# A hybrid encoder on one Trainium2 core: conv taps into PSUM, and a new order and engine table for the mixer's steps

## The chip, the cores and the metric

One core of one Trainium2 chip. The time is device microseconds of one launch; lower is better. Before the change three runs gave 2029.0, 2029.43 and 2029.79 us, median 2029.43.

## The reference

`x` is 512 tokens by 1024 channels, and there are two layers. Each layer does

```
x += 1/2 SwiGLU_1(RMSNorm(x))                       # d_ff 2816
h  = RMSNorm(x) @ W_in                              # 1696 columns
y  = concat[ MLA(h_mla), Conv(h_conv), Hyena(h_hy) ] # each group RMS-normalised
x += y @ W_out
x += 1/2 SwiGLU_2(RMSNorm(x))
```

MLA is attention with 8 heads over latent projections (softmax over 512 keys). Conv is `a * sigmoid(g)`, a depthwise convolution of 31 taps over 256 channels, a layer norm and a silu. Hyena is a depthwise convolution of 3 taps over 768 channels, then two long filters as products with spectra, each followed by a gate. A last RMSNorm ends it. All is float32.

## The kernel before

Channels lie on partitions and the 512 tokens on the free axis, so `x` is eight tiles of 128x512. Float32 products are made from parts: a matrix is split into a rounded part `hi` (a cast on ScalarE, L327) and a remainder `lo` (a subtraction on VectorE, L301, or on GpSimd, L331), and a product is three TensorE passes, hi·hi, hi·lo and lo·hi (`mm3`, L366 to L368). Each weight tile is loaded raw by SyncE's queue (`load_w`, `wr`), then cast (`wh`) and subtracted (`wl`).

The program is written as a list of operations. `Plan.issue` (L176) is a list scheduler: it runs a clock over modelled costs, gives each engine the ready operation that was written first, and lets a tile take a buffer only when one is free. The order that results is fixed for each engine, and on the chip each engine works through its own list in order, waiting at semaphores. The costs are those in `v_tt`, `v_stt`, `act`, `p_tt`, `mm` and so on (L299 to L383); each engine counts for itself. PSUM is one tag, `ps`, of 8 banks. Other work tiles share one tag of 61 slots.

`mixer` (L818) writes its steps in the order of `MIX_ORDER` (L30). `C` makes a half of the conv's input (two `W_in` tiles, then `upad`), `H` one of Hyena's six input tiles with its short convolution (`short_conv`, L697), `K`, `Q`, `KV`, `W` and `V` the latents of attention, `S` a head's scores and softmax, `P` its values, `Y` a piece of the long filters (`long_conv`, L706), `T` a number of conv taps (`conv_taps`, L774), `CF` and `HF` the norms of the conv and Hyena groups, `OM` and `OR` the two halves of the output projection, which add into `x`.

Of the 62 first-stage taps of a layer, 33 run on VectorE (2 `v_ts` that start `cacc` and 31 `v_stt` that add into it, all in SBUF); the other 29, those in `POOL_TAPS`, are a ScalarE scaling into `tap` (L322) and a GpSimd addition (L331). Hand-made tables (`POOL_W`, `POOL_Y`, `POOL_WIN`, `ACT_NORM` and so on, L33 to L40) say which other operations go to GpSimd or ScalarE.

Of the kernel before, what the change touches and what calls it, by code (L numbers as in the profile page):

```python
# [19 lines left out]
P = 128  # L20
# [28 lines left out]
# columns of the packed per-layer vectors  # L49
# [8 lines left out]
# columns of the packed constants  # L58
# [6 lines left out]
class Tile:  # L65
    """a tile that is allocated when the first operation that writes it is issued"""
# [10 lines left out]
class View:  # L77
    """a tile, or an access pattern of DRAM, behind a chain of slices that is applied when it is issued"""
# [44 lines left out]
class Op:  # L123
    """one step of the program"""

    __slots__ = ("engine", "cost", "emit", "succ", "n_pred", "ready", "index", "allocs", "tiles", "table", "late", "prio", "start", "end",
                 "crit")
# [5 lines left out]
class Plan:  # L133
    def __init__(self, nc):
        self.nc, self.ops, self.tags, self.prio = nc, [], {}, 0
# [5 lines left out]
    def add(self, engine, cost, emit, reads, writes, table=None, late=0.0, after=()):  # L141
        op = Op()
        op.engine, op.cost, op.emit, op.table, op.late = engine, cost, emit, table, late
# [30 lines left out]
        self.ops.append(op)  # L174

    def issue(self):  # L176
        """list schedule by rank among what is ready; a tile leaves a slot for every earlier tile of its tag"""
        events, ready, seq = [], {}, 0
# [22 lines left out]
        while done < len(self.ops):  # L201
# [15 lines left out]
            for engine, heap in ready.items():  # L217
# [24 lines left out]
                end = now + cost  # L242
                op.start, op.end = now, end
# [19 lines left out]
def trunk(ctx: ExitStack, tc: tile.TileContext, a: dict, out: bass.AP):  # L263
# [35 lines left out]
    def v_tt(o, x0, x1, op):  # L299
        plan.add("DVE", 0.07 + o.free * 1.04e-3,  # L300
                 lambda: nc.vector.tensor_tensor(out=g(o), in0=g(x0), in1=g(x1), op=op), rd(x0, x1), [o])  # L301

    def v_ts(o, x0, s1, s2_, op0, op1=None):
        c = 1.1e-3 if x0.in_psum else 0.52e-3
        kw = {} if op1 is None else {"op1": op1}
        plan.add("DVE", 0.07 + o.free * c + 0.06 * len(rd(s1, s2_)),
                 lambda: nc.vector.tensor_scalar(out=g(o), in0=g(x0), scalar1=g(s1), scalar2=g(s2_), op0=op0, **kw),  # L307
                 rd(x0, s1, s2_), [o])

    def v_stt(o, x0, s, x1, op0, op1):  # L310
        plan.add("DVE", 0.07 + o.free * 1.04e-3 + 0.06 * len(rd(s)),
                 lambda: nc.vector.scalar_tensor_tensor(out=g(o), in0=g(x0), scalar=g(s), in1=g(x1), op0=op0, op1=op1),  # L312
                 rd(x0, s, x1), [o])

    def v_copy(o, x0):
        plan.add("DVE", 0.07 + o.free * (1.04e-3 if x0.in_psum else 0.52e-3),
                 lambda: nc.vector.tensor_copy(g(o), g(x0)), rd(x0), [o])
# [11 lines left out]
    def p_tt(o, x0, x1, op):  # L329
        plan.add("POOL", 0.06 + o.free * 2.3e-3,  # L330
                 lambda: nc.gpsimd.tensor_tensor(out=g(o), in0=g(x0), in1=g(x1), op=op), rd(x0, x1), [o])  # L331

    def p_ts(o, x0, s1, s2_, op0, op1):
        plan.add("POOL", 0.06 + o.free * 1.3e-3,
                 lambda: nc.gpsimd.tensor_scalar(out=g(o), in0=g(x0), scalar1=g(s1), scalar2=g(s2_), op0=op0, op1=op1),
                 rd(x0, s1, s2_), [o])

    def p_pow(o, x0, x1):
        plan.add("POOL", 1.0, lambda: nc.gpsimd.tensor_tensor(out=g(o), in0=g(x0), in1=g(x1), op=ALU.pow),  # L339
                 rd(x0, x1), [o])  # L340
# [11 lines left out]
    def mm(o, lhs, rhs, start, stop, passes=4):  # L352
        plan.add("PE", rhs.free * passes / 2.4e3 + 0.003,
# [5 lines left out]
    def mm3(o, pairs):  # L359
        """sum of lhsT.T @ rhs over (lhs_hi, lhs_lo, rhs_hi, rhs_lo), three passes each"""  # L360
# [10 lines left out]
        for i, p in enumerate(pairs):  # L371
            plan.add("PE", 3 * (p[2].free / 2.4e3 + 0.003), emit(i, *p), list(p), [o])

    def mm2(o, pairs):
        """sum of lhsT.T @ (rhs_hi + rhs_lo) over (lhs, rhs_hi, rhs_lo)"""
# [34 lines left out]
    def load_w(src, width, pool_lo=False):  # L410
        """raw weights [128, width] to their f32r parts"""
# [3 lines left out]
        (p_tt if pool_lo else v_tt)(lo[:, :width], raw[:, :width], hi[:, :width].f, ALU.subtract)  # L415
# [5 lines left out]
    def stat(t, n, eps):  # L421
        """sum over partitions / n + eps, as [token % 128, token // 128]"""
# [9 lines left out]
    def bcast(c, n=4):  # L432
        """[128, n] by token to a PSUM row of 128 n in every partition"""
# [14 lines left out]
    def squares(tiles):  # L448
        acc = None
        for t in tiles:  # L450
# [4 lines left out]
            else:  # L455
                p_tt(acc, acc, sq, ALU.add)
        return acc

    class Norm:
        """takes x tiles as they become final; gives the split x * g and the row 1 / rms"""  # L460
# [3 lines left out]
        def __init__(self, l, name):  # L464
            self.l, self.name, self.xh, self.xl, self.acc, self.squared = l, name, [], [], None, 0

        def add(self, k, square=True):
# [4 lines left out]
            self.xh.append(h)  # L472
            self.xl.append(lo)
# [3 lines left out]
        def square(self, k):  # L477
            self.squared = k + 1
# [4 lines left out]
            else:  # L483
                p_tt(self.acc, self.acc, sq, ALU.add)

        def pairs(self, wt):
            return [(h, lo, self.xh[k], self.xl[k]) for k, (h, lo) in enumerate(ktiles(wt, KD))]

        def row(self):
            for k in range(self.squared, KD):  # L490
                self.square(k)
            return rstd_row(self.acc, D)

    def reduce_angle(t):
        """t to [-pi, pi], in place"""
# [27 lines left out]
    def down_in_halves(src, gh, gl, nxt):  # L523
        """the last product, by halves of the tokens; the weights stay for the second one"""
# [27 lines left out]
    def ffn(l, which, nrm, nxt, filler=None, first=None):  # L552
# [3 lines left out]
        def evac(pg, pu, gh, gl):  # L556
# [5 lines left out]
            p_tt(s, s, rb[0], ALU.mult)  # L562
# [30 lines left out]
    def spectra(l, res):  # L593
        """puts (ka, kc, inv) into res: spectra [block][order] of [j, kind, channel] and 1 / (512 sum |k|) by channel"""
# [12 lines left out]
        def packed(t):  # L607
            """t, twice in its rows, as [hi; lo]"""
# [27 lines left out]
        for par_ in range(2):  # L636
# [7 lines left out]
            for c in range(2):  # L644
# [10 lines left out]
                for op in (ALU.add, ALU.subtract):  # L655
                    t, th, tl = s2(s="sd"), s2(F32R, "sh"), s2(F32R, "sl")
                    p_tt(t, fb[0], fb[1], op)
# [5 lines left out]
                p_tt(fb[0], fb[0], fb[1], ALU.add)  # L663
                if ch:
                    p_tt(nrm, nrm, fb[0], ALU.add)
# [40 lines left out]
    def long_conv(l, o, u, gate, spec, res):  # L706
        """puts gate * (u (*) k + d u) for the two channel tiles into res"""
        ka, kc, iv = spec
        xp = [ps(), ps()]
        for t in range(2):  # L710
# [3 lines left out]
            p_tt(ue, up, dn_, ALU.add)  # L714
            v_tt(uo[:, 0::2], up[:, 0::2], dn_[:, 0::2], ALU.subtract)
            v_tt(uo[:, 1::2], dn_[:, 1::2], up[:, 1::2], ALU.subtract)
# [7 lines left out]
        wh, wl = [], []  # L724
        for jb in range(2):
# [11 lines left out]
            p_tt(m1.halves(), m1.halves(), m2.halves()[:, ::-1], ALU.subtract)  # L737
            v_tt(m3, ab, kcj, ALU.mult)
            v_tt(m4.halves(), cd.halves(), kaj.halves()[:, ::-1], ALU.mult)
            p_tt(m3.halves(), m3.halves(), m4.halves()[:, ::-1], ALU.add)  # L740
            w0, w1 = s2(s="w"), s2(s="w")
            (p_tt if 2 * o + jb in POOL_W0 else v_tt)(w0[:, 0:256], m1[:, 0:256], m1[:, 256:512], ALU.add)
            v_tt(w0[:, 256:512], m1[:, 0:256], m1[:, 256:512], ALU.subtract)
            p_tt(w1[:, 0:256], m3[:, 256:512], m3[:, 0:256], ALU.add)
            p_tt(w1[:, 256:512], m3[:, 256:512], m3[:, 0:256], ALU.subtract)
            wh.append([s2(F32R, "wsh") for _ in range(2)])
            wl.append([s2(F32R, "wsl") for _ in range(2)])
# [509 lines left out]
```

## Time and profile before

| | us |
|---|---|
| median of three runs | 2029.43 |
| span of the profiled execution, first to last instruction | 2025.7 |
| TensorE matmuls busy in it | 1938.7 |
| VectorE busy | 1161.0 |
| ScalarE busy | 778.9 |
| GpSimd busy | 674.3 |

The profile gives no other time of that execution than its span; 3.7 us of the median lie outside of it. Busy time is an average over very unlike stages: most of the span is feed-forward, and each layer has one mixer, at about 387 to 651 us and at 1387 to 1651 us. A view by stage says more than these totals. A matmul's row shows its whole passage (about 0.39 us), while the next starts after 0.23 us, so rates are better read from counts in a stretch than from durations. VectorE's instructions overlap in the same way, by about 0.08 us.

### The profile page before, as it was taken

How to read it: one execution, taken by the hardware profiler on the slowest of the kernel's cores; microseconds unless marked ns; L12 is line 12 of the kernel's file. 1: busy time of each engine (PE TensorE's matmuls, PEld its weight loads, DVE VectorE, ACT ScalarE, POOL GpSimd, SP SyncE). 2: the span in 40 equal slices, each digit the busy share in tenths (PEclk: the TensorE clock that was granted, in tenths of full speed). 3: DMA queues.
4: the chain of work that ended last, by engine and by line, in shares of the span. 5: the costliest groups of instructions: out<-in, count | busy, mean ns of one | idle time of the engine just before them, and what ended most of it. 6: DMA issues, size and time to landing. Idle time of an engine off the chain costs nothing. (4 is left out here: it accounts for less than half of the span.)

```text
span 2025.7 us, 22874 instructions
## 1 busy us (share of the span) xinstructions
PE 1938.7 (96%) x8880; PEld 1600.4 (79%) x8880; DVE 1161.0 (57%) x1478; ACT 778.9 (38%) x1183; POOL 674.3 (33%) x494
## 2 busy tenths in 40 slices
PE   8999999977999999999999999999769999999998
PEld 6888888865787888888888888888558878888888
DVE  7545633498997443433567364345988874334352
ACT  5323312443785322322433232234348743222133
POOL 4204301278777110101214041014786851011012
PEclk9999999988999999999999999999879999999999
DMA  7333222311003333333433323323200133333341
GB/s 238 100 106 110 88 94 81 107 58 52 1 16 115 94 94 102 96 94 98 130 96 96 123 83 93 95 83 96 69 28 1 32 120 95 103 95 94 100 119 43
DMA packets 58301, 179.10 MB, mean 88 GB/s; under 512 B 6608, under 2 KB 10704, under 8 KB 58192
## 3 DMA queue, kind: packets, MB, share of 16 engines
q1 hardware_dynamic: 55312, 172.66, 27.9%
q0 software_dynamic: 2880, 4.98, 0.9%
q8 instruction: 69, 1.13, 0.2%
q14 instruction: 40, 0.33, 0.1%
HBM read 175.52 MB, written 2.10 MB: 88 GB/s over the span
## 5 line engine op out<-in xcount | busy, mean ns | idle before, releaser
L327 ACT CAST wh<-wr 128x1024 fp32r<-128x1024 f32 (+2 forms) x328 | 324.5, 991 | 946.5 <-PE ps L367 647.9
L366 PE MATMUL ps<-xh,wh 128*128 128x512 f32 x1600 | 627.0, 392 | 0.0
L368 PE MATMUL ps<-xh,wl 128*128 128x512 f32 x1600 | 624.7, 390 | 0.7 <-DVE wl L301 0.7
L367 PE MATMUL ps<-xl,wh 128*128 128x512 f32 x1600 | 624.6, 390 | 0.8 <-DVE xl L312 0.8
L331 POOL TENSOR_TENSOR s<-s,rb 128x512 f32<-128x512 f32 x88 | 153.3, 1744 | 1010.4 <-ACT s L322 1010.4
L301 DVE TENSOR_TENSOR wl<-wr,wh 128x1024 fp32r<-128x1024 f32 (+1 forms) x282 | 357.3, 1267 | 46.0 <-ACT wh L327 38.1
L367 PEld LDWEIGHTS ps<-xl,wh 128*128 128x128 f32 x1600 | 301.5, 188 | 64.4 <-DVE xl L312 1.6
L368 PEld LDWEIGHTS ps<-xh,wl 128*128 128x128 f32 x1600 | 301.4, 188 | 64.0 <-DVE wl L301 1.1
L366 PEld LDWEIGHTS ps<-xh,wh 128*128 128x128 f32 x1600 | 301.5, 188 | 62.2 <-issue 0.5
L367 PE MATMUL ps<-gl,wh 128*128 128x512 f32 x656 | 255.2, 389 | 0.0
L366 PE MATMUL ps<-gh,wh 128*128 128x512 f32 x656 | 255.2, 389 | 0.0
L368 PE MATMUL ps<-gh,wl 128*128 128x512 f32 x656 | 255.2, 389 | 0.0
L301 DVE TENSOR_TENSOR g<-ps,s 128x512 f32<-128x512 f32 x88 | 60.9, 692 | 250.1 <-PE ps L368 234.4
L312 DVE SCALAR_TENSOR_TENSOR x<-ps,x 128x512 f32<-128x512 f32 x88 | 60.9, 692 | 237.2 <-PE ps L368 237.2
L301 DVE TENSOR_TENSOR s<-ps,rb 128x512 f32<-128x512 f32 x88 | 60.8, 691 | 195.9 <-PE ps L368 185.7
L367 PEld LDWEIGHTS ps<-gl,wh 128*128 128x128 f32 x656 | 123.1, 188 | 25.7
L368 PEld LDWEIGHTS ps<-gh,wl 128*128 128x128 f32 x656 | 123.2, 188 | 25.5
L366 PEld LDWEIGHTS ps<-gh,wh 128*128 128x128 f32 x656 | 123.1, 188 | 25.4
L331 POOL TENSOR_TENSOR sq<-sq,sq 128x512 f32<-128x512 f32 (+1 forms) x62 | 85.1, 1373 | 135.6 <-ACT sq L322 130.7
L331 POOL TENSOR_TENSOR tap<-tap,tap 128x512 f32<-128x512 f32 x54 | 90.0, 1671 | 14.4 <-ACT tap L322 12.2
L312 DVE SCALAR_TENSOR_TENSOR cacc<-upad,par,cacc 128x512 f32<-128x512 f32 x62 | 85.9, 1386 | 1.1
L331 POOL TENSOR_TENSOR wl<-wr,wh 128x512 fp32r<-128x512 f32 (+1 forms) x44 | 78.6, 1789 | 13.6 <-ACT wh L327 13.5
(258 smaller groups left out, 2409.2 us busy)
## 6 DMA issues: line engine op xcount, KB each, us to landing
wr<-in_gu SPq DMA_DIRECT2D x174, 512.0 KB, 3.6
wr<-in_dn SPq DMA_DIRECT2D x64, 512.0 KB, 3.5
wr<-in_win SPq DMA_DIRECT2D x28, 512.0 KB, 3.6
wr<-in_dn SPq DMA_DIRECT2D x32, 384.0 KB, 3.1
wr<-in_wout SPq DMA_DIRECT2D x32, 256.0 KB, 2.6
x<-in_xT SPq DMA_DIRECT2D x8, 256.0 KB, 5.2
mat<-in_spec POOLq DMA_DIRECT2D x8, 256.0 KB, 4.9
wr<-in_wqb SPq DMA_DIRECT2D x4, 512.0 KB, 3.6
```

The costliest lines, as they stand in the source:

```text
L301: lambda: nc.vector.tensor_tensor(out=g(o), in0=g(x0), in1=g(x1), op=op), rd(x0, x1), [o])
L312: lambda: nc.vector.scalar_tensor_tensor(out=g(o), in0=g(x0), scalar=g(s), in1=g(x1), op0=op0, op1=op1),
L327: plan.add("ACT", 0.06 + o.free * 0.86e-3, lambda: nc.scalar.copy(out=g(o), in_=g(x0)), rd(x0), [o])
L331: lambda: nc.gpsimd.tensor_tensor(out=g(o), in0=g(x0), in1=g(x1), op=op), rd(x0, x1), [o])
L366: nc.tensor.matmul(oo, lhsT=h, rhs=x0, start=(i == 0), stop=False)
L367: nc.tensor.matmul(oo, lhsT=h, rhs=x1, start=False, stop=False)
L368: nc.tensor.matmul(oo, lhsT=lo, rhs=x0, start=False, stop=(i == n - 1))
```

## The change

- The taps of the short list are all on VectorE. `conv_taps` becomes one generator for each of the two channel tiles; it accumulates into a PSUM bank, `ps()`, and only the last tap writes SBUF.
- `short_conv` scales its projection in place in PSUM and reads it there (before: a copy in SBUF, `hu`). `out_mla` scales its product in place in PSUM (before: a tile `om`), and `out_mla` and `out_rest` become steps by output tile.
- `values` always adds a head's two halves by one VectorE operation out of PSUM.
- The scheduler gets a flag `port` on VectorE operations whose operands are all in SBUF and on GpSimd's arithmetic; two such operations follow one another in the modelled clock. A matmul's modelled cost becomes that of its columns plus 32.
- The tables are replaced by one, `SECOND`: inside the mixer an operation that may run on VectorE or GpSimd (`e_tt`), or on ScalarE or GpSimd (`e_scaled`), takes the second engine where its number stands under its step. Outside the mixer each such operation stays where it was.
- `MIX_ORDER` is new. Heads need not come in order. The first long filter takes its second block first. Buffer counts, layouts and the data loaded stay.

```diff
+MIX_ORDER = ("C0 A10 K C1 H0 B1 Q A1 H1 A2 H3 A6 B1 A2 B1 Y1 B2 H5 Y1 B2 A1 B1 Y1 B3 A2 B2 A2 KV B2 A1 B1 A1 B1 H2 "
+             "H4 A2 B1 Y1 W B1 Y1 B2 S2 B1 S0 Y1 S1 B1 Y1 B2 S4 V S5 B1 S3 Y1 P0 B2 P1 P4 P2 S6 Y1 B1 S7 B1 P3 P6 "
+             "P5 P7 CF Y1 OM0 OM5 OM4 OM2 OM7 HF OM3 OR0 OM6 OM1 OR1 OR2 OR3 OR4 OR5 OR6 OR7")
+SECOND = ("C0:0 H1:0 C1:2 Q:0124 H3:0 H2:0 H0:0 H4:0 KV:01 Y0:02345 Y2:0134567 Y1:01234567 W:012 S0:23 S1:01 "
+          "Y4:0 Y5:12345 S2:124 Y6:0124567 S3:012 P1:0 Y7:0123467 S4:023 P3:01 S5:0124 S6:0134 S7:1234 Y9:0 "
+          "P5:01 HF:1 CF:034 OM3:0 OM4:0 OM6:0 OR1:01 OR2:1 OR3:01 OR4:1 OR6:1 OR7:01")
...
                 end = now + cost
+                if op.port:
+                    end = free = max(now, free) + cost
...
     def v_stt(o, x0, s, x1, op0, op1):
...
-                 rd(x0, s, x1), [o])
+                 rd(x0, s, x1), [o], port=not (x0.in_psum or x1.in_psum))
...
+    def e_tt(o, x0, x1, op, default=1):
+        if x0.in_psum or x1.in_psum or o.in_psum:
+            return v_tt(o, x0, x1, op)
+        plan.either([("DVE", 0.07 + o.free * 1.04e-3,
...
+                     ("POOL", 0.06 + o.free * 2.3e-3,
...
     def short_conv(l, t, p, rb):
-        u, o = s2(s="hu"), s2(s="ho")
+        u, o = p, s2(s="ho")
         v_tt(u, p, rb, ALU.mult)
...
+    def conv_taps(l, t, res, fed):
+        acc = ps()
+        v_ts(acc, upad[t][:, 0:S], pc(l, "dw", 31 * t), pc(l, "dwb", t), ALU.mult, ALU.add)
+        for j in range(1, 31):
+            to = s2(s="cacc") if j == 30 else acc
+            v_stt(to, upad[t][:, j:j + S], pc(l, "dw", 31 * t + j), acc, ALU.mult, ALU.add)
...
             yl = s2(s="yl")[0:64]
             a_copy(yl, p[64:128])
-            if h in POOL_Y:
-                a_copy(ypair[r], p[0:64])
-                p_tt(ypair[r], ypair[r], yl, ALU.add)
-            else:
-                v_tt(ypair[r], p[0:64], yl, ALU.add)
+            v_tt(ypair[r], p[0:64], yl, ALU.add)
...
-                t = s2(s="om")
-                v_tt(t, p, row, ALU.mult)
-                v_tt(x[d], x[d], t, ALU.add)
+            v_tt(p, p, lat["row"], ALU.mult)
+            into_x(d, p)
...
+        def into_x(d, p):
+            v_tt(x[d], p, x[d], ALU.add)
```

`A` and `B` are taps of the first and the second channel tile, `Y` the pieces of the long filters; a number behind them counts pieces, and `SECOND` numbers the pieces of `Y` from 0 to 9.

## Rows read from the trace of the kernel before

**Rows 1.** The page: span and busy time of each engine.
```profile
span 2025.7 us, 22874 instructions
PE 1938.7 (96%) x8880; PEld 1600.4 (79%) x8880; DVE 1161.0 (57%) x1478; ACT 778.9 (38%) x1183; POOL 674.3 (33%) x494
```

**Rows 2.** Busy time by stretch; the first line names the columns.
```profile
core 0: us, PE busy (x) PEld busy (x) DVE busy (x) ACT busy (x) POOL busy (x), PEclk, DMA share, GB/s
407.00:505.00 98.00, 71.74 (x293) 56.99 (x292) 90.18 (x83) 41.95 (x62) 77.13 (x45) 0.84 0.19 57
505.00:598.00 93.00, 89.50 (x499) 74.09 (x498) 84.29 (x173) 76.67 (x165) 72.82 (x73) 1.00 0.03 9
598.00:651.00 53.00, 48.48 (x225) 38.69 (x224) 44.06 (x53) 28.34 (x44) 40.65 (x29) 1.00 0.29 85
750.00:775.00 25.00, 25.00 (x112) 20.71 (x111) 9.59 (x10) 5.27 (x5) 0.00 (x0) 1.00 0.32 96
1407.00:1505.00 98.00, 71.56 (x291) 56.35 (x290) 90.82 (x84) 41.16 (x61) 77.43 (x46) 0.84 0.18 56
```

**Rows 3.** Waits of TensorE, 407 to 598 us: total, times, longest.
```profile
PE ps L357 <- POOL sq L331: 10.8, 1, 10.8
PE ps L357 <- ACT sq L322: 6.1, 1, 6.1
PE ps L357 <- DVE fold L301: 4.5, 2, 3.8
```

**Rows 4.** Timeline of VectorE, 405 to 440 us: start, us, what.
```profile
411.85 0.68 DVE L301 TENSOR_TENSOR am<-ps,rb 128x512 f32<-128x512 f32 x1
412.45 8.19 DVE L312 SCALAR_TENSOR_TENSOR cacc<-upad,par,cacc 128x512 f32<-128x512 f32 x5
...
421.16 0.74 DVE L312 SCALAR_TENSOR_TENSOR cacc<-upad,par,cacc 128x512 f32<-128x512 f32 x1
421.82 1.22 DVE L301 TENSOR_TENSOR wl<-wr,wh 128x1024 fp32r<-128x1024 f32 x1
```

**Rows 5.** Timeline of GpSimd over the same stretch.
```profile
410.01 4.79 POOL L331 TENSOR_TENSOR tap<-tap,tap 128x512 f32<-128x512 f32 x3 [1.45 <-ACT tap L322]
...
417.57 1.74 POOL L331 TENSOR_TENSOR tap<-tap,tap 128x512 f32<-128x512 f32 x1
421.99 2.20 POOL L331 TENSOR_TENSOR upad<-am,gm 128x512 f32<-128x512 f32 x1 [2.68 <-ACT gm L322]
```

**Rows 6.** VectorE's groups, 407 to 598 us: count, busy, mean ns, idle before.
```profile
L312 DVE SCALAR_TENSOR_TENSOR cacc<-upad,par,cacc 128x512 f32<-128x512 f32 x31 | 42.9, 1385 | 0.5
...
L312 DVE SCALAR_TENSOR_TENSOR ho<-hu,par,ho 128x511 f32<-128x511 f32 x12 | 15.4, 1280 | 2.3 <-ACT ho L322 2.2
...
L301 DVE TENSOR_TENSOR wl<-wr,wh 128x1024 fp32r<-128x1024 f32 x5 | 8.2, 1635 | 0.0
L301 DVE TENSOR_TENSOR ql<-qf,qh 128x512 fp32r<-128x512 f32 x6 | 5.8, 966 | 0.2
...
L301 DVE TENSOR_TENSOR fold<-ho 128x128 f32<-128x128 f32 x4 | 4.2, 1084 | 0.0
...
L301 DVE TENSOR_TENSOR w<-m 128x256 f32<-128x256 f32 x4 | 2.3, 583 | 0.0
...
L307 DVE TENSOR_SCALAR cacc<-upad,par 128x512 f32<-128x512 f32 x2 | 2.0, 1014 | 0.0
...
L301 DVE TENSOR_TENSOR fold<-hy 128x128 f32<-128x128 f32 x4 | 1.5, 398 | 0.0
L301 DVE TENSOR_TENSOR wsl<-w,wsh 128x512 fp32r<-128x512 f32 x2 | 1.4, 751 | 0.0
```

**Rows 7.** GpSimd's groups, 407 to 598 us.
```profile
L331 POOL TENSOR_TENSOR tap<-tap,tap 128x512 f32<-128x512 f32 x27 | 45.0, 1670 | 7.3 <-ACT tap L322 6.2
...
L331 POOL TENSOR_TENSOR wl<-wr,wh 128x1024 fp32r<-128x1024 f32 x5 | 13.2, 2646 | 0.0
...
L331 POOL TENSOR_TENSOR ypair<-ypair,yl 64x512 f32<-64x512 f32 x6 | 7.7, 1286 | 8.8 <-ACT ypair L327 8.6
```

**Rows 8.** ScalarE's group of scaled taps, 407 to 598 us.
```profile
L322 ACT ACTIVATE tap<-upad,par 128x512 f32<-128x512 f32 x29 | 18.7, 711 | 0.7 <-POOL upad L331 0.7
```

**Rows 9.** VectorE's groups over the whole span.
```profile
L312 DVE SCALAR_TENSOR_TENSOR x<-ps,x 128x512 f32<-128x512 f32 x88 | 60.9, 692 | 237.2 <-PE ps L368 237.2
...
L301 DVE TENSOR_TENSOR gl<-g,gh 128x512 fp32r<-128x512 f32 x88 | 60.3, 685 | 3.5 <-ACT gh L327 3.4
```

**Rows 10.** VectorE's groups, 598 to 651 us.
```profile
L301 DVE TENSOR_TENSOR x<-x,om 128x512 f32<-128x512 f32 x8 | 9.9, 1258 | 0.1
```

**Rows 11.** Waits of TensorE, 598 to 651 us.
```profile
PE ps L357 <- POOL r L339: 3.3, 2, 1.8
```

More of the change, by code (lines that the diff above doesn't have):

```diff
@@ L60, with words @@
 NCC = 9
+def words(text):
+    n = {"A": 0, "B": 0, "Y": 0}
+    for word in text.split():
+        if word[0] in n:
+            for _ in range(int(word[1:])):
+                yield f"{word[0]}{n[word[0]]}"
+                n[word[0]] += 1
+        else:
+            yield word
 class Tile:
@@ L139, in tile, with add @@
         return View(t)
-    def add(self, engine, cost, emit, reads, writes, table=None, late=0.0, after=()):
+    def add(self, engine, cost, emit, reads, writes, table=None, late=0.0, after=(), port=False):
         op = Op()
-        op.engine, op.cost, op.emit, op.table, op.late = engine, cost, emit, table, late
+        op.engine, op.cost, op.emit, op.table, op.late, op.port = engine, cost, emit, table, late, port
+        op.ways, op.word = None, self.word
         op.succ, op.n_pred, op.ready, op.index, op.allocs = [], 0, 0.0, len(self.ops), []
@@ L174, in add, with either @@
         self.ops.append(op)
+        return op
+    def either(self, ways, reads, writes, default):
+        n = default
+        if self.word is not None:
+            k = self.free_choice[self.word] = self.free_choice.get(self.word, -1) + 1
+            n = 1 if k in SECOND.get(self.word[1], ()) else 0
+        engine, cost, emit, port = ways[n]
+        op = self.add(engine, cost, emit, reads, writes, port=port)
+        if self.word is not None:
+            op.ways = k, ways, default
     def issue(self):
-        events, ready, seq = [], {}, 0
+        events, ready, seq, free = [], {}, 0, 0.0
         busy, table = {}, None
@@ L483, in square @@
             else:
-                p_tt(self.acc, self.acc, sq, ALU.add)
+                e_tt(self.acc, self.acc, sq, ALU.add)
         def pairs(self, wt):
-            return [(h, lo, self.xh[k], self.xl[k]) for k, (h, lo) in enumerate(ktiles(wt, KD))]
+            w = ktiles(wt, KD)
+            return [(*w[k], *self.x[k]) for k in self.x]
         def row(self):
-            for k in range(self.squared, KD):
-                self.square(k)
+            for k in self.x:
+                if k not in self.squared:
+                    self.square(k)
             return rstd_row(self.acc, D)
@@ L723, in long_conv @@
         yield 1
-        wh, wl = [], []
-        for jb in range(2):
+        wh, wl = {}, {}
+        for jb in ((1, 0) if o == 0 else (0, 1)):
             bank = []
@@ L832, in scaled @@
             return t
-        u, yc, hy, hqs, vv, lat = [], {}, {}, [], [], {}
+        u, yc, hy, hqs, vv, lat = {}, {}, {}, [], [], {}
         fed = set()
-        taps = conv_taps(l, u, fed)
+        taps = [conv_taps(l, t, u, fed) for t in range(2)]
         def conv_in(t):
@@ L858, in rope_key @@
             p = ps()
[L859 removed]
+            mm2(p, [(wk[:, k], *nrm.x[k]) for k in nrm.x])
             km = scaled(p, "km")
[L861 removed]
+            e_tt(km, km, cs, ALU.mult)
             pr = ps()
@@ L948, in values @@
             pair, odd = h // 2, h % 2
-            assert len(ym) == pair and ("y" in st or not odd)
             probs = st.pop(h)
@@ new lines, in into_x, with out_rest, out_mla @@
+        def into_x(d, p):
+            v_tt(x[d], p, x[d], ALU.add)
+            done.append(d)
+            if done.count(d) == 2:
+                nxt.add(d)
+        def out_rest(d):
+            both = yc["conv"] + yc["hy"]
+            wt = load_w(a["wout"][l, d, :, 512:1024], 512)
+            p = ps()
+            mm3(p, [(*w, *both[k]) for k, w in enumerate(ktiles(wt, 4))])
+            into_x(d, p)
+        def out_mla(d):
+            assert len(ym) == 4
+            wt = load_w(a["wout"][l, d, :, 0:512], 512)
+            p = ps()
+            mm3(p, [(*w, *ym[k]) for k, w in enumerate(ktiles(wt, 4))])
+            if "row" not in lat:
+                lat["row"] = rstd_row(st["acc"], 512)
+            v_tt(p, p, lat["row"], ALU.mult)
+            into_x(d, p)
```

191 lines of the change are left out of this document (76 added, 115 removed).

## The prediction

> **What bounds the kernel now.** I read the page first: TensorE is busy 96% of the span [rows 1]. That alone would say that only fewer matmuls help, and the change removes none. So I read busy time by stretch next, with cuts where the kind of matmul changes. A feed-forward stretch starts 112 matmuls in 25 us [rows 2]. The first part of the mixer, 407 to 505 us (the front), starts 293 in 98 us; at the feed-forward rate those take 293/112 x 25 = 65.4 us, so 32.6 are lost: 26.3 idle, the rest because the granted clock averages 0.84 there, about a third of the stretch at the lower of its two levels, 1.2 GHz, behind those idle times. The heads' part, 505 to 598, loses 3.5 us, the out part, 598 to 651, 4.5 [rows 2]. That is 40.6 us for each mixer, and the second one has the same front [rows 2]. Two times 40.6 is all there is to win: 2029.4 - 81 = 1948.
>
> Third, who is full there: VectorE, 90.2 of 98 us and 84.3 of 93, together 174.5 of 191 (91%) [rows 2]. TensorE's waits in these parts name GpSimd's and ScalarE's squares and VectorE's folds [rows 3]: one wait of 10.8 us, one of 6.1, two of 4.5. They are late links of chains that run through VectorE and GpSimd, while TensorE, in order, has other products queued behind.
>
> Fourth, why VectorE is full. Two timelines side by side: while GpSimd adds taps from 410.01 on, five VectorE taps need 8.19 us, 1.64 each; with GpSimd idle, from 419.3 to 421.99, one takes 0.74, and the next instruction starts 0.66 after it [rows 4, 5]. A multiplication that reads one operand from PSUM took 0.68 in the middle of GpSimd's taps [rows 4]. GpSimd's multiplication that met VectorE's subtraction took 2.20 [rows 5]. So operations with both operands in SBUF and GpSimd's take turns, and a PSUM operand frees VectorE from it. 31 taps cost 1385 ns each, 12 short-convolution additions 1280 [rows 6].
>
> **The change, part by part**, for one mixer, on VectorE, in the 191 us before the out part. Where a whole instruction comes or goes I take 0.08 off its duration, the overlap of 0.74 and 0.66.
>
> *Taps.* 31 taps at 1385 go, 31 x 1.305 = 40.5 us, and two starting ones of 2.0. 60 come whose accumulator is read from and written to PSUM. No row has a VectorE write into PSUM. From below, 0.69 for a PSUM read [rows 9] with an SBUF write; from above, the taps of today at 1.38 [rows 6]. I take 0.75, the 0.69 with the lone tap's [rows 4] extra of 0.05 for its per-partition scalar, since that row differs only in where the result goes: 60 x 0.67 = 40.2, the starts about 1.3. Change: -1. So twice the taps at the same VectorE time; what is gained is 18.7 us of ScalarE [rows 8] and 45 us of GpSimd [rows 7].
>
> *Short convolution.* 12 additions drop from 1.28 to the lone tap's 0.74: 12 x 0.54 = -6.5. The in-place scaling writes PSUM, bounded as above.
>
> [...]
>
> *Moved to GpSimd.* Weight remainders: five were on VectorE here, 8.2 us [rows 6]; four of the 13 input tiles are left on it in all, say three in this stretch at 1.22 [rows 4]: -4.5. Folds: 4.2 + 1.5 [rows 6] become two, 0.7: -5. Remainders of queries six to three, pieces of the filters' products 2.3 to three of 0.42, their remainders 1.4 to none [rows 6]: 9.5 to 3.3, -6.
>
> *Moved to VectorE.* `km`, one `upad`, one of `te`/`to`, two gates, the last pair's square and sum: seven at 0.685; six more head sums at 0.69 [rows 9]. 13 x 0.61 = +8. The seven have both operands in SBUF and meet GpSimd; +0.5 each for about half of them, +2, against -1 for what stays and meets less.
>
> Sum: -1 - 6.5 - 4.5 - 5 - 6 + 8 + 1 = -14; 174.5 becomes 160.5. GpSimd loses 45.0 + 7.7 [rows 7] and gains some 25 (six weight remainders at 2.65 [rows 7], the rest small): from 150 [rows 2] to some 125, so it does not become the bound; ScalarE had 42 and 77 [rows 2] and loses.
>
> *Order.* The `B` taps reach to the seventh head: work whose operands are always there, placed where VectorE idled 8.7 of 93 us [rows 2]. And the scheduler now delays in its clock what is delayed on the chip, so TensorE's list should no longer hold a transpose 10.8 us early [rows 3]. I let a third of VectorE's 16.5 idle us go: 160.5 + 11 = 171.5 for 191. TensorE needs 65.4 + 89.5 = 155 there, so it doesn't bind yet. Weight loads move with their steps on SyncE's queue; the DMA share is 0.19 and 0.03 [rows 2], so nothing of it shows; were a load late, its step would be.
>
> *Out part.* 8 additions into `x` drop from 1.26 [rows 10] to 0.69, -4.6; 10 of 16 weight remainders come from GpSimd to VectorE, 10 x 0.61 = +6; VectorE is at 44 of 53 [rows 2] and stays under TensorE's 48.5. `OM` ahead of `HF` and steps by tile may hide part of the 3.3 us in which TensorE waits for a norm's power [rows 11]: -2.
>
> Elsewhere engines stay; the modelled cost of matmuls changes the order in feed-forward, where TensorE is at 25.00 of 25 [rows 2]: nothing, and if that cover went, VectorE with 9.59 of 25 would still keep up.
>
> Per mixer -19.5 - 2, two mixers -43; from the profiled execution's 2025.7 [rows 1] to 1982.7, and with the 3.7 us that the median lies above it about 1986.
>
> **The rivals.** *TensorE becomes the bound.* If VectorE's list fills as well as the scheduler can count it, the 191 us shrink to TensorE's 155 and the out part by 2: -38 each, 2029 - 76 = 1953. For it: 160.5 on VectorE is near 155. Against: two engines that full seldom wait for nothing.
>
> *A new wait takes half.* Two of the eight banks are held through front and heads, and nine of 13 weight remainders wait for GpSimd at 2.65 instead of 1.2. Against: a head's score block holds a bank for some 2.2 us, an estimate from three matmuls of 0.22 [rows 2] and two readers at PSUM's 0.69 [rows 9] with waits between, so six banks should do. If VectorE's idle time rises by 10 us instead of falling by 5.5, a mixer wins 6: 2017.
>
> *Slower: PSUM writes cost.* If VectorE writes PSUM, or reads and writes one bank, at half rate, an instruction of 512 columns takes the 1.22 of one with 1024 [rows 4], +0.53. 74 write there (the 2 starts, 58 taps, all but the last of each tile, 6 scalings, 8 output scalings): 39 us more, against 21.5 won, +17.5 a mixer: 2064. It decides from 21.5/74 = 0.29 us more an instruction, a tap of 1.04. For it: no row shows such a write. Against: reading PSUM costs 7 ns.
>
> *The change does not do what it says:* the chip's order of arrivals differs from the scheduler's clock still, and stalls of the size of those in [rows 3] come at other places, 20 us a mixer, as before: 2029. Against: in the trace the turn-taking explains both late engines.
>
> **How the numbers follow.** Forecast 0.54, 1986 (1970 to 2005 by idle time of 3 to 20 us); TensorE bound 0.18; half taken 0.13; PSUM writes 0.10; no effect 0.05. The range reaches from the TensorE floor, 1950, to the half-taken case, 2018; above lie the last two, 0.15. Faster by over 0.2% (4 us, about what a measurement of this kernel can tell from no change): 0.54 + 0.18 + 0.13 = 0.85; same 0.05; slower 0.10.
>
> **What would show it.** Taps into PSUM at 0.72 to 0.80 and their count 116 for the two layers; `ho` at 0.75; `tap` gone; the front-and-heads stretch of one mixer near 171 us with VectorE over 93%; no wait of TensorE over 4 us; the granted clock in the front above 0.9. It is wrong if taps take over 1 us, if GpSimd or a PSUM bank is what TensorE waits for, or if VectorE's share falls below 88%.

## The result and the profile after

The changed kernel takes 1958.91 us (median of four runs, 1956.76 to 1960.02) against 2029.22 for the kernel before beside it: 0.9652 of it [0.9638, 0.9666], 70.3 us less. The forecast was 1986.0, so the sign and the range held and the size did not: 70 us against 43. The forecast's own case ran from 1970 to 2005; the result lies below it, 6 us from the rival in which TensorE becomes the bound (1953), and it is that rival's floor that brought it into the range.

The page of the changed kernel, span and engines, then the row of the granted clock over 40 slices; they answer to [rows 1]:

```profile
span 1956.2 us, 22760 instructions
PE 1922.1 (98%) x8880; PEld 1593.0 (81%) x8880; DVE 1113.3 (57%) x1550; ACT 740.4 (38%) x1119; POOL 534.0 (27%) x416
...
PEclk9999999999999999999999999999999999999999
```

The matmuls are as many as before; TensorE is busy 16.6 us less, as next to nothing runs at the lower clock any more (granted clock over the span 0.998 against 0.983), and idle 53 us less (1956.2 - 1922.1 = 34.1 against 87.0). VectorE has lost 48 us of work, GpSimd 140.

Read along TensorE's timeline, the 69.5 us between the two spans lie in the mixers alone. Up to the first mixer's first product the changed kernel needs 391.7 us against 387.0, so **4.7 more**; the first mixer 229.4 against 264.3 (-34.9), the part between the mixers 734.1 against 734.8 (-0.7), the second mixer 227.2 against 265.4 (-38.2), the rest 373.9 against 374.2 (-0.3).

Busy time by stretch, columns as in [rows 2]. The first mixer now has its front at 411 to 486, its heads at 486 to 574 and its out part at 574 to 621; the second mixer's front and heads follow:

```profile
411.00:486.00 75.00, 74.28 (x361) 61.88 (x360) 73.75 (x114) 29.36 (x40) 49.44 (x36) 1.00 0.24 74
486.00:574.00 88.00, 81.26 (x436) 65.51 (x435) 82.62 (x167) 72.23 (x158) 49.32 (x52) 1.00 0.03 10
574.00:621.00 47.00, 47.00 (x224) 38.97 (x224) 41.68 (x66) 27.32 (x44) 22.90 (x17) 1.00 0.33 101
1374.00:1449.00 75.00, 74.29 (x360) 61.88 (x359) 73.75 (x118) 28.91 (x39) 50.35 (x37) 1.00 0.25 74
1449.00:1535.00 86.00, 80.93 (x437) 65.63 (x436) 80.28 (x163) 72.45 (x159) 48.76 (x51) 1.00 0.03 10
```

Front and heads take 163 us where they took 191. TensorE idles 0.7 and 6.7 us there (26.3 and 3.5 before), and not at all in the out part (4.5 before). The granted clock in the front is 1.00, against 0.84: with the 26 us of idle time the stretches at the lower level behind it have gone too. That level was 0.50, granted from 435 to 446 us and from 490 to 500 us of the kernel before, with 1.00 from 465 to 487 us between them; with the mean of 0.84 that makes a third of the front. Four rows of TensorE's timeline of the kernel before at 425 to 470 us, two at each level, show products of 512 columns that start 0.43 us apart at the lower level and 0.23 at the full one:

```profile
444.76 0.63 PE L381 MATMUL ps<-xh,wh 128*128 128x512 f32 x1
445.19 0.63 PE L382 MATMUL ps<-xl,wh 128*128 128x512 f32 x1
...
447.14 0.40 PE L381 MATMUL ps<-xh,wh 128*128 128x512 f32 x1
447.37 0.40 PE L382 MATMUL ps<-xl,wh 128*128 128x512 f32 x1
```

The profile gives the clock as a share of full speed and not in GHz; the prediction's 1.2 is, in it, 512 columns in 0.43 us, 1.2 a ns. In the changed kernel VectorE is busy 73.75 of 75 and 82.62 of 88: both engines are now full, which is why the result comes near the rival's time.

TensorE's waits at 380 to 640 us, to be held against [rows 3] and [rows 11]:

```profile
PE ps L413 <- DVE ql L365: 2.7, 2, 1.4
PE ps L411 <- ACT qh L354: 1.7, 2, 1.0
PE ps L413 <- POOL ql L367: 0.7, 2, 0.4
PE ps L402 <- POOL sq L367: 0.7, 1, 0.7
```

The waits of 10.8, 6.1 and 4.5 for squares and folds are gone but for 0.7, and the 3.3 for a norm's power with them. What is left is mostly for the queries' parts, 1.4 us at a time at most.

VectorE's groups at 407 to 598 us, which answer to [rows 6] (count, busy, mean ns, idle before):

```profile
L339 DVE SCALAR_TENSOR_TENSOR ps<-upad,par,ps 128x512 f32<-128x512 f32 x58 | 41.7, 745 | 0.3
...
L339 DVE SCALAR_TENSOR_TENSOR ho<-ps,par,ho 128x511 f32<-128x511 f32 x12 | 8.8, 737 | 0.0
...
L327 DVE TENSOR_TENSOR ps<-ps,rb 128x512 f32<-128x512 f32 x12 | 8.2, 691 | 0.9 <-PE ps L413 0.6 <-ACT rb L354 0.3
...
L334 DVE TENSOR_SCALAR ps<-upad,par 128x512 f32<-128x512 f32 x2 | 1.6, 812 | 0.0
...
L339 DVE SCALAR_TENSOR_TENSOR cacc<-upad,par,ps 128x512 f32<-128x512 f32 x2 | 1.5, 736 | 0.0
```

58 taps that read and write a bank take 745 ns each, the two that write SBUF 736, and the short convolution's additions 737: the lone tap of [rows 4] had 0.74. All 60 taps with their starts cost 44.8 us (41.7 + 1.6 + 1.5), what 31 and two starts cost before (42.9 + 2.0).

VectorE's and GpSimd's timelines at 460 to 475 us (start, us, what) show why, as [rows 4, 5] did for the kernel before:

```profile
466.29 2.05 DVE L339 SCALAR_TENSOR_TENSOR ps<-upad,par,ps 128x512 f32<-128x512 f32 x3
468.26 0.68 DVE L472 TENSOR_REDUCE c<-ps 128x4 f32<-128x512 f32 x1
```

```profile
464.77 2.74 POOL L367 TENSOR_TENSOR wsl<-w,wsh 128x512 fp32r<-128x512 f32 x2
467.46 1.31 POOL L367 TENSOR_TENSOR m<-m,m 128x512 f32<-128x512 f32 x1
```

Three taps take 2.05 us, 0.66 from one to the next (the instruction behind them starts 1.97 after the first), as the lone tap of [rows 4] did, while GpSimd adds and subtracts beside them at 1.31 and 1.37 each. Neither is seen to wait for the other.

The 4.7 us at the start stand in TensorE's and GpSimd's timelines at 12 to 24 us (brackets: the wait ahead of it):

```profile
17.18 0.40 PE L413 MATMUL ps<-xh,w0l 128*128 128x512 f32 x1
21.33 0.80 PE L402 MATMUL ps<-ident,sq 128*128 128x128 f32 x4 [3.75 <-POOL sq L367]
21.78 0.78 PE L411 MATMUL ps<-xh,w0h 128*128 128x512 f32 x1
```

```profile
14.73 6.54 POOL L367 TENSOR_TENSOR sq<-sq,sq 128x512 f32<-128x512 f32 x4 [0.86 <-ACT sq L349]
```

ScalarE's last cast of a first weight part, from its timeline at 5 to 26 us:

```profile
14.49 0.60 ACT L354 CAST w0h<-w 128x512 fp32r<-128x512 f32 x1
```

TensorE holds the transposes of the first norm's squares in its list ahead of products of the second weight tile, and GpSimd's sums of those squares end at 21.27. The product that stands behind them could have run, for its rounded weights were there at 15.09. Behind the wait the granted clock is 0.50 from 22 to 24 us. Before, the order was the other way round and no such wait is there. The likely cause is the planner, by the matmuls' cost or the flag `port`; runs below tell the two apart.

### The profile page after: what moved, and what is told of

Its sections match the earlier page's. It is cut to its first block, busy times and chain, and to the rows that moved or that the text cites. A ratio compares the mean times of both kernels' runs of the same rounds, so it can differ in the third digit from the quotient of the medians.

```text
span 1956.2 us, 22760 instructions
## 1 busy us (share of the span) xinstructions
PE 1922.1 (98%) x8880; PEld 1593.0 (81%) x8880; DVE 1113.3 (57%) x1550; ACT 740.4 (38%) x1119; POOL 534.0 (27%) x416
## 4 chain that ended last, share of the span: by engine, by line
PE 85%; DVE 10%; ACT 3%; issue 1%; POOL 0%; DMA 0%; SPq 0%; POOLq 0%; DVEq 0%; ACTq 0%
PE ps L411 28%; PE ps L413 28%; PE ps L412 28%; DVE ps L339 3%; DVE ptl L327 1%; DVE mx L970 1%; ACT p L349 1%; PE ps L402 1%; DVE kl L327 1%; ACT p L373 1%; PE ps L426 0%; DVE ho L339 0%; PE ps L427 0%; ACT kh L354 0%; PE ps L399 0%
## 5 line engine op out<-in xcount | busy, mean ns | idle before, releaser
L365 DVE TENSOR_TENSOR wl<-wr,wh 128x1024 fp32r<-128x1024 f32 (+2 forms) x290 | 351.8, 1213 | 53.1 <-ACT wh L354 44.7
L367 POOL TENSOR_TENSOR sq<-sq,sq 128x512 f32<-128x512 f32 x44 | 63.9, 1451 | 122.1 <-ACT sq L349 121.8
L367 POOL TENSOR_TENSOR wl<-wr,wh 128x1024 fp32r<-128x1024 f32 (+1 forms) x36 | 75.3, 2094 | 50.9 <-ACT wh L354 48.9
L339 DVE SCALAR_TENSOR_TENSOR ps<-upad,par,ps 128x512 f32<-128x512 f32 x116 | 83.5, 745 | 0.6
L365 DVE TENSOR_TENSOR gl<-g,gh 128x512 fp32r<-128x512 f32 x88 | 61.4, 698 | 4.1 <-ACT gh L354 4.1
```

## The experiments

Four things go in together: operands that move to PSUM, 29 taps and the heads' sums that move to VectorE, a new order with a new table, and a scheduler with other knowledge. The theory behind the forecast is that VectorE's turn-taking with GpSimd is what went, through the PSUM operands; the rivals give the gain to the order and the table, to the flag `port`, or to the matmuls' new cost. The port that some expectations speak of, twice as shared, is what the flag stands for in the planner's clock: the runs show that VectorE's operations on SBUF take longer beside GpSimd's (four taps in SBUF 4.87 us, and 2.72 with GpSimd idle), and no run shows what of the hardware the two share. Every ratio is against the kernel before, run beside it. The changed kernel stands at 0.9652.

### The changed kernel with one part undone

**Taps accumulate in SBUF.**

```diff
     def conv_taps(l, t, res, fed):
-        acc = ps()
+        acc = s2(s="cacc")
```

> The changed kernel with one part undone: the taps accumulate in SBUF instead of a PSUM bank; all 60 stay on VectorE, order and table stay, the scheduler is told of the port. Theory 1 (the gain is VectorE's release from taking turns with GpSimd): a tap rises from 0.745 us to about 1.3, 30 us more VectorE a mixer, 2005 to 2025 us. Theory 2 (the gain is the new order and the scheduler's knowledge, which would plan around it): taps below 0.95, 1965 to 1980 us.

Measured: 2018.29 us, 0.9948 [0.9933, 0.9963], 59 us of the 70 lost and in the range of Theory 1. VectorE's taps at 390 to 650 us:

```profile
L339 DVE SCALAR_TENSOR_TENSOR cacc<-upad,par,cacc 128x512 f32<-128x512 f32 x60 | 72.5, 1233 | 0.1
```

The same taps in the same order of steps cost 1233 ns instead of 745. Times 60 that is 29 us a mixer, and twice that the 59 us.

This run also settles a rival: that a running sum in SBUF is slow by itself, because each tap needs the result of the one before. Two rows of VectorE's timeline at 452 to 484 us, and then GpSimd's over the same stretch (the bracket gives its idle time):

```profile
455.85 2.72 DVE L339 SCALAR_TENSOR_TENSOR cacc<-upad,par,cacc 128x512 f32<-128x512 f32 x4
...
460.84 4.87 DVE L339 SCALAR_TENSOR_TENSOR cacc<-upad,par,cacc 128x512 f32<-128x512 f32 x4
```

```profile
460.82 3.01 POOL L367 TENSOR_TENSOR wl<-wr,wh 128x1024 fp32r<-128x1024 f32 x1 [6.97 <-ACT wh L354]
```

Four taps in a row in SBUF take 2.72 us while GpSimd is idle (453.85 to 460.82), as quick as in PSUM, and four more take 4.87 once it subtracts beside them.

**Short convolution and output scaling in SBUF.**

```diff
-        u, o = p, s2(s="ho")
+        u, o = s2(s="hu"), s2(s="ho")
...
-            v_tt(p, p, lat["row"], ALU.mult)
-            into_x(d, p)
+            t = s2(s="om")
+            v_tt(t, p, lat["row"], ALU.mult)
+            into_x(d, t)
```

> The changed kernel with the short convolution's scaled input and the output's scaled product back in SBUF; taps stay in PSUM. 20 operations a mixer have two SBUF operands again, at 0.75 to 1.25 us. Theory 1: up to 6 us a mixer before the output, up to 4 in it, where TensorE bounds: 1962 to 1975 us. Theory 3: the planner, which knows the port, hides it, 1956 to 1964 us.

Measured: 1999.48 us, 0.9854 [0.9839, 0.9869]: 41 us back, far above what either theory gave. The additions themselves, at 390 to 650 us:

```profile
L339 DVE SCALAR_TENSOR_TENSOR ho<-hu,par,ho 128x511 f32<-128x511 f32 x12 | 13.9, 1166 | 0.4 <-ACT ho L349 0.4
```

They explain 5.1 us a mixer (13.9 - 8.8), near the 6.5 in the sum of the prediction; yet the stretch up to the out part is 18 us longer. VectorE has 11.6 us more work in it, and 6.4 more idle time; other operations on SBUF got longer too, such as ten weight remainders of 128x512 at 390 to 650 us, 1068 ns each against 876 in the changed kernel. So a price read off the instruction alone undercounts what an undone part costs here.

**The order of before**, with what else is new:

```diff
-MIX_ORDER = ("C0 A10 K C1 H0 B1 Q A1 H1 A2 H3 A6 B1 A2 B1 Y1 B2 H5 Y1 B2 A1 B1 Y1 B3 A2 B2 A2 KV B2 A1 B1 A1 B1 H2 "
...
+MIX_ORDER = ("C0 H1 A16 C1 A5 Q H3 A5 K H2 A1 H0 H4 H5 A3 B11 KV B19 Y4 W S0 S1 Y1 "
+             "V Y1 P0 S2 Y1 S3 P1 Y1 P2 S4 P3 S5 S6 Y1 S7 Y2 P4 P5 P6 P7 HF CF "
+             "OM0 OM1 OM2 OM3 OM4 OM5 OM6 OM7 OR0 OR1 OR2 OR3 OR4 OR5 OR6 OR7")
```

> The changed kernel with the order of steps of the kernel before (its T steps as taps of the first, then of the second channel tile); table, PSUM taps and port stay. Theory 1: at most 10 us a mixer lost, 1960 to 1978 us. Theory 2: most of the gain lost, 1990 to 2015 us, with VectorE's idle time above 15 us a mixer.

Measured: 1992.21 us, 0.9817 [0.9802, 0.9832], in the range of Theory 2: 33 us back, though that is under half of the gain and not most of it. TensorE's longest wait at 380 to 660 us:

```profile
PE ps L411 <- ACT wsh L354: 9.6, 1, 9.6
```

**The table of before**, `SECOND` rewritten so that each step gets the engines of the old tables:

```diff
-SECOND = ("C0:0 H1:0 C1:2 Q:0124 H3:0 H2:0 H0:0 H4:0 KV:01 Y0:02345 Y2:0134567 Y1:01234567 W:012 S0:23 S1:01 "
...
+SECOND = ("C0:2 C1:02 Q:1234 H0:0 K:0 W:012 Y0:03 Y5:03 Y1:01245 Y2:0124567 Y6:0124567 Y7:0124567 Y3:0 Y4:0 Y8:0 Y9:0 "
...
```

> The changed kernel with the engine choices of the kernel before for all that is not a tap or a head's sum; order, PSUM taps and port stay. About 30 more operations with both operands in SBUF stand on VectorE in each mixer (folds, weight remainders). Theory 1: each costs 0.7 to 1.2 us there, 10 to 20 us a mixer, 1980 to 2000 us. Theory 2: the scheduler finds room, 1960 to 1975 us.

Measured: 2006.30 us, 0.9883 [0.9867, 0.9900], 47 us back and above both ranges. TensorE waits 9.5 us for the same `wsh` as in the run before.

**The scheduler does not know of the turn-taking:**

```diff
-        op.table, op.late, op.port = engine, cost, emit, table, late, port
+        op.table, op.late, op.port = engine, cost, emit, table, late, False
```

> The changed kernel, but the scheduler's clock ignores the shared port; order, table and PSUM taps stay. Theory 1: few VectorE operations with both operands in SBUF are left, so the knowledge is worth little, 1952 to 1968 us (the start, which lost 4.7 us, may come back). Theory 2: early transposes stall TensorE again by 10 us and more in each front, 1980 to 2000 us.

Measured: 1977.54 us, 0.9743 [0.9728, 0.9757], between the theories: 19 us back. The first mixer begins at 388.4 us, so the flag is what moved most of the start; the mixers are some 10 us longer each.

**The matmuls' cost of before:**

```diff
-        plan.add("PE", 0.24 if rhs.free == 1 else (rhs.free + 32) * passes / 2.4e3,
+        plan.add("PE", rhs.free * passes / 2.4e3 + 0.003,
...
```

with the same in `mm3` and `mm2`.

> The changed kernel with the old modelled cost of matmuls (0.65 us for three of 512 columns instead of 0.68), all else as changed. Theory 1: TensorE's own cost moves few decisions, 1957 to 1966 us. Theory 4 (the order and table are tuned to one plan, and any other plan from the same words loses): 1970 to 1990 us.

Measured: 1982.70 us, 0.9763 [0.9749, 0.9778], the range of Theory 4: 24 us back, by a number that no instruction carries, through the order that comes out of it.

Busy time of these runs from the first mixer's begin to its out part (columns as in [rows 2]). The kernel before:

```profile
387.00:598.00 211.00, 181.25 (x882) 147.64 (x881) 181.98 (x265) 126.28 (x235) 155.21 (x121) 0.93 0.13 40
```

The changed kernel:

```profile
391.00:574.00 183.00, 175.55 (x887) 143.92 (x886) 164.10 (x290) 109.01 (x206) 104.22 (x92) 1.00 0.15 47
```

Taps in SBUF:

```profile
391.00:605.00 214.00, 184.59 (x885) 149.49 (x884) 190.71 (x290) 109.16 (x205) 112.58 (x92) 0.94 0.13 40
```

Short convolution and output scaling in SBUF:

```profile
391.00:592.00 201.00, 184.50 (x889) 149.13 (x888) 175.70 (x290) 110.25 (x206) 106.70 (x92) 0.95 0.14 43
```

The order of before:

```profile
391.00:585.00 194.00, 176.79 (x885) 145.56 (x884) 168.21 (x291) 107.44 (x203) 103.37 (x92) 0.96 0.14 43
```

The table of before:

```profile
391.00:597.00 206.00, 186.28 (x888) 151.25 (x887) 171.82 (x301) 108.65 (x203) 92.76 (x84) 0.93 0.13 42
```

Without the flag:

```profile
388.00:579.00 191.00, 179.06 (x882) 145.20 (x881) 162.09 (x289) 109.22 (x205) 103.55 (x92) 0.98 0.14 44
```

The matmuls' cost of before:

```profile
392.00:585.00 193.00, 180.88 (x884) 147.19 (x883) 166.33 (x289) 109.17 (x205) 102.46 (x92) 0.96 0.14 44
```

Take VectorE's busy time (the third pair) from the length of the stretch. Undoing the PSUM taps costs work: 190.7 against 164.1, and idle time rises by only 4 (23.3 against 18.9). Undoing a part of the planning costs idle time: 25.8 with the old order, 34.2 with the old table, 28.9 without the flag, 26.7 with the old matmul cost, with work of -2 to +8. Undoing the short convolution and the output scaling costs both, 11.6 of work and 6.4 of idle time. So the PSUM taps and the planning act mainly on different terms of VectorE's time. But the six prices, 59 + 41 + 33 + 47 + 19 + 24 = 223 us, are three times the gain: the parts hang together, and what one costs when undone is not what it brought.

### The kernel before with one part added

That question needs the opposite experiments, on the order, the tables and the costs of before.

**Taps of before, accumulators in PSUM**, the split between the engines kept:

```diff
-            acc = s2(s="cacc")
+            acc = ps()
...
-                    v_stt(acc, upad[t][:, j:j + S], pc(l, "dw", 31 * t + j), acc, ALU.mult, ALU.add)
+                    to = s2(s="cacc") if j == 28 else acc
+                    v_stt(to, upad[t][:, j:j + S], pc(l, "dw", 31 * t + j), acc, ALU.mult, ALU.add)
+                    acc = to
```

> The kernel before with one part done: VectorE's 31 taps accumulate in a PSUM bank, all else (29 taps on ScalarE and GpSimd, order, table, planner) as it was. Theory 1 (VectorE's turns with GpSimd are the price, and come back as time): a tap 0.745 instead of 1.386, 20 us less VectorE a mixer, 1988 to 2000 us. Theory 3 (found from the undone parts: VectorE's idle time, which the order sets, counts as much as its work): half of it turns into idle time, 2003 to 2018 us.

Measured: 1994.93 us, 0.9830 [0.9814, 0.9847], the range of Theory 1: half the gain, 34 us, with nothing else changed. Its taps at 388 to 585 us:

```profile
L312 DVE SCALAR_TENSOR_TENSOR ps<-upad,par,ps 128x512 f32<-128x512 f32 x29 | 21.7, 748 | 0.5
...
L312 DVE SCALAR_TENSOR_TENSOR ho<-hu,par,ho 128x511 f32<-128x511 f32 x12 | 17.3, 1442 | 1.3 <-ACT ho L322 1.3
```

The short convolution, left in SBUF, takes longer than before (1442 against 1280 [rows 6]); that it meets GpSimd more is the likely cause and is not shown.

**All taps on VectorE as well**, `POOL_TAPS` empty:

```diff
-POOL_TAPS = (9, 10, 11, 12, 13, 16, 21, 23, 24, 25, 26, 27, 29, 30, 32, 36, 38, 40, 42, 45, 46, 47, 49, 51, 54, 56, 58, 60, 61)
+POOL_TAPS = ()
...
-            acc = s2(s="cacc")
+            acc = ps()
...
+                    to = s2(s="cacc") if j == 30 else acc
...
```

> The kernel before with all 60 taps on VectorE in PSUM and none on ScalarE and GpSimd; order, table and planner as they were. VectorE's tap time stays near 43 us a mixer, GpSimd loses 48, what is left on VectorE with two SBUF operands waits less. Theory 1: 12 to 20 us less VectorE a mixer, 1990 to 2006 us. Theory 3: the old order leaves VectorE idle, 2006 to 2022 us.

Measured: 2003.53 us, 0.9875 [0.9860, 0.9889], inside the range of Theory 1, yet 8.6 us worse than with the old split. In the old order the other 29 taps fill VectorE (171.7 busy up to the out part, against 166.5) more than GpSimd's freedom is worth.

**The planner's flag alone**: `port` is set on the same operations, and the two engines' flagged operations follow one another in its clock.

```diff
                 end = now + cost
+                if op.port:
+                    end = free = max(now, free) + cost
```

> The kernel before, whose scheduler alone is told of the shared port; order of steps, table and taps as they were. Theory 1: VectorE's work stays, so 2015 to 2030 us. Theory 2 (the scheduler's knowledge is the gain): the 10.8 and 6.1 us waits go, 1990 to 2010 us. The start loses some 4 us as in the changed kernel.

Measured: 2056.33 us, 1.0134 [1.0119, 1.0149]: 27 us **slower**, outside both ranges. TensorE's longest group of waits at 380 to 660 us, and what is left of those for squares:

```profile
PE ps L371 <- DVE wl L303: 17.9, 3, 8.6
...
PE ps L360 <- ACT sq L325: 1.1, 1, 1.1
```

The waits of 10.8 and 6.1 for squares did go, as Theory 2 had it and as the forecast's sentence on early transposes said; but waits for weight remainders, 17.9 us in all, came in their place, and the sum is worse. With the order and the table that it had, the planner makes a worse list when it counts the turn-taking.

**All PSUM operands, nothing else**: the edit of the first run of this group, with the short convolution and the output scaling in place.

```diff
-        u, o = s2(s="hu"), s2(s="ho")
+        u, o = p, s2(s="ho")
...
-                t = s2(s="om")
-                v_tt(t, p, row, ALU.mult)
-                v_tt(x[d], x[d], t, ALU.add)
+                v_tt(p, p, row, ALU.mult)
+                v_tt(x[d], p, x[d], ALU.add)
```

> The kernel before with all operands moved to PSUM and nothing else: the 31 taps of VectorE accumulate in PSUM, the short convolution's and the output's scalings are in place in PSUM. Old order, old table, old planner, 29 taps still on ScalarE and GpSimd. Over the run with the taps alone (1994.9) 12 additions drop by 0.5 us and 8 by 0.57 in each mixer. Theory A (the release of VectorE carries over in any order): 9 to 11 us a mixer less, 1973 to 1978 us. Theory B (beyond the taps the old order leaves the gain as idle time): 1984 to 1995 us.

Measured: 1968.84 us, 0.9695 [0.9678, 0.9711], below both ranges: **60 of the 70 us**, in the old order, with the old tables and the old scheduler. Its stretch up to the out part and its out part:

```profile
388.00:573.00 185.00, 177.50 (x885) 145.44 (x884) 156.01 (x265) 126.11 (x235) 145.80 (x121) 0.98 0.14 46
573.00:624.00 51.00, 48.94 (x228) 39.15 (x227) 39.46 (x53) 28.69 (x45) 38.10 (x29) 1.00 0.31 91
```

and two groups of the first, VectorE's additions and GpSimd's:

```profile
L312 DVE SCALAR_TENSOR_TENSOR ho<-ps,par,ho 128x511 f32<-128x511 f32 x12 | 8.9, 741 | 1.3 <-ACT ho L322 1.2
```

```profile
L331 POOL TENSOR_TENSOR tap<-tap,tap 128x512 f32<-128x512 f32 x27 | 38.1, 1425 | 2.1 <-ACT tap L322 1.4
```

TensorE's longest wait at 380 to 660 us:

```profile
PE ps L357 <- ACT sq L322: 1.8, 1, 1.8
```

So the waits of 10.8, 6.1 and 4.5 of [rows 3] go without a new order and without the flag: what was late was late because of the turn-taking. VectorE's 182.0 us become 156.0, with 29.0 idle as before. GpSimd gains as well: its taps take 1425 ns against 1670 [rows 7]. Against this kernel the full change has 8 us more work on VectorE, 10 less idle, 42 less on GpSimd, an out part of 47 instead of 51 us, and a start that is 3.1 us later (391.7 against 388.6). So the 29 taps and the heads' sums on VectorE, order, table and planner together are worth about 10 us (1968.84 to 1958.91), and two out parts that are 3 to 4 us shorter are the larger part of it.

### The start

**The first norm's sums of squares later in the planner's clock**, so that the transposes fall behind the second weight tile in TensorE's list:

```diff
+            elif (self.l, self.name) == (0, "ffn1"):
+                acc = self.acc
+                plan.add("POOL", 0.06 + S * 2.3e-3, (lambda: nc.gpsimd.tensor_tensor(
+                    out=g(acc), in0=g(acc), in1=g(sq), op=ALU.add)), [acc, sq], [acc], late=0.6, port=True)
             else:
                 e_tt(self.acc, self.acc, sq, ALU.add)
```

> The changed kernel with one number more in its planner: in the first norm, GpSimd's sums of squares count as available 0.6 us later each, so TensorE's transposes of that sum stand behind the first two weight tiles instead of ahead of the second. Theory: the 3.75 us wait at the start and the half clock behind it go, 3.5 to 5 us less, 1954 to 1956 us. Rival (the start's order only moves the wait): 1958 to 1960 us.

Measured: 1957.22 us (1953.07 to 1959.12), 0.9640 [0.9626, 0.9654]. The wait is gone and the first mixer begins at 388.3 us, but the intervals of the two kernels overlap: 3.4 us of the start are had back in the trace, and no faster total is shown.

**The flag in the mixers alone:**

```diff
-        op.table, op.late, op.port = engine, cost, emit, table, late, port
+        op.table, op.late, op.port = engine, cost, emit, table, late, port and self.word is not None
```

> The changed kernel with the planner's port flag only for operations of the mixer; the feed-forward parts and the start are planned without it. Theory: the start comes back (4.7 us) and the mixers stay, 1953 to 1957 us. Rival: the mixers' plan hangs on what goes ahead of it, and shifts there cost 5 us or more a mixer, 1962 to 1975 us.

Measured: 1957.78 us, 0.9645 [0.9630, 0.9659]: the mixer begins at 388.4 and its stretch stays at 183 us, and again the total is not told apart from the change. The cause of the later start is thus the flag outside the mixers for 3.3 of the 4.7 us; the rest is open, and the kernel before with all PSUM operands and no flag begins at 388.6 too. No version is shown to beat the changed kernel.

## Why the prediction was right, and where its sizes were off

*The bound and the mechanism* were right. VectorE was the engine to relieve, and the operand in PSUM relieves it: with the whole of the rest as before, that alone gives 60 us. The reading behind it, five taps at 1.64 beside GpSimd against one at 0.74 without it [rows 4, 5], gave 0.75 for the new tap; 745 ns were measured. (The 1.64 is a mixed price: the five taps also met a weight's remainder and, at their end, an idle GpSimd [rows 5].) Three taps in a bank took 2.05 us beside GpSimd's work, where four in SBUF took 4.87. What the forecast named as the gain of the taps, 45 us of GpSimd and 18.7 of ScalarE, was worth little: the kernel before with all PSUM operands keeps the 29 taps on both engines and has 60 of the 70 us.

*Taps, short convolution, weights, folds*: -1, -6.5, -4.5 and -5 were forecast. From the groups come 44.9 to 44.8 us of taps in 29 more instructions, which at 0.08 of overlap each is -2.3; 15.4 to 8.8; 8.2 to 3.7; 5.7 to 0.7. The remainders and pieces fell from 9.5 to 5.3, less than the -6. VectorE's busy time fell from 174.5 to 156.4 (73.75 + 82.62), by 18 instead of 14. The 4 us that lack are about what is left for the term "contention +1", which then had the wrong sign. That what stays on VectorE with both operands in SBUF meets a GpSimd that works 99 us and not 150 would explain it, but it is not shown: some of these operations got shorter (the remainders of queries from 966 ns [rows 6] to 796), others longer (the pieces of the filters' products from 583 to 951).

*GpSimd at 125* was 26 us too high (49.44 + 49.32 = 98.8). The forecast took off the taps and the head sums and forgot the operations that it had just moved to VectorE and the sums that go with the taps, some 14.5 us of gates, rotations and sums, and had all others at their contended durations.

*Order* is, with the out part, the step that was most undersized: a third of VectorE's 16.5 idle us was let go, and 9.9 went (1.25 + 5.38 = 6.6 are left of 163). The -28 of this stretch are thus 8.5 more than forecast, in equal parts from work and from idle time. The doubt behind the third, that two engines that full seldom wait for nothing, was wrong here. The step's reason was also too narrow: it gave the end of the 10.8 us wait to the scheduler's knowledge, and with PSUM operands alone that wait is gone in the old list. (The waits for folds are 4.5 us for the two together [rows 3], not each.)

*Out part*: -2 was forecast for the hidden wait and 6 were had, 53 to 47 us with TensorE busy throughout; the wait of [rows 11] went wholly.

*Elsewhere nothing* was wrong by +4.7. The prediction looked at feed-forward in its steady state, where TensorE is full, and not at its first microseconds, where few weight tiles are there yet and the planner's choice decides. For 3.3 us of it the flag is the cause, as two runs show.

Summed: the first mixer -34.9 and the second -38.2 in place of -21.5 each, and the start +4.7.

*The rivals.* PSUM writes at half rate is refuted by the 745 ns. Nothing waits for a bank in the longest waits, so the new wait did not come. "TensorE becomes the bound" is nearly what happened: its floor of 155 us was not reached (163), its out part was passed (47 where it had 51). "The change does not do what it says" is refuted by the 70 us.

*What a bank costs:* taps in PSUM took 745 ns against the lone tap's 0.74 us, and scalings in place 691 against 685 for a subtraction in SBUF [rows 9]. The 7 ns that the prediction gives for a read are 692 against 685 [rows 9].

*What was argued and is not shown:* that order, table, flag and matmul cost were fitted to each other. The runs show that undoing one of these costs 19 to 47 us and that the flag alone in the old kernel costs 27. Not tried: an order and a table made for the old split of the taps with PSUM operands, which GpSimd's 104 us of 183 leave room for.

## What to carry to other kernels

Where VectorE and GpSimd work side by side, give VectorE's running sums and in-place steps a PSUM bank if one is free: the same instruction went from 1233 to 745 ns, and in the kernel before GpSimd's additions of taps beside it went from 1670 to 1425. What stays in SBUF on VectorE can get longer by it (1280 to 1442 ns for the short convolution), so move all that have a bank. Undo a part to see what the rest now leans on, but add it alone to the old kernel to see what it brings: here the undone parts summed to 223 us of a gain of 70, while one kind of edit alone gave 60. And when a scheduler's costs are changed, its order and tables may no longer fit: the flag alone made the old kernel 1.3% slower, and taking it out of the changed kernel cost 19 us.

## What the runs showed of the hardware that was not expected

A VectorE instruction that reads and writes the same bank costs what it costs in SBUF without GpSimd beside it (745 ns for 512 columns, against the lone tap's 0.74 us [rows 4]). The tap that starts a sum is the exception: as a tensor-scalar from SBUF it took 0.54 undisturbed, the first line below from VectorE's timeline of the kernel before at 407 to 598 us, and 812 ns into PSUM.

```profile
409.03 0.54 DVE L307 TENSOR_SCALAR cacc<-upad,par 128x512 f32<-128x512 f32 x1
```

With four starts in the kernel that is 1.1 us of VectorE against undisturbed starts in SBUF; beside GpSimd those of the kernel before had taken 1014 ns on average [rows 6]. And the contention was worth more than the instructions that were moved: setting 12 additions and some scalings a mixer back into SBUF cost 5.1 us in the additions, but 18 in the stretch.
